# Probabilities of three attentions split in SBUF and turned by DMA, in pieces of 512 columns

## The chip, the cores and the metric

The kernel runs on one core of a Trainium2 chip. The metric is the device time of one execution in microseconds (us), from launch to the end. Engines named below: PE (TensorE, matrix products), DVE (VectorE), ACT (ScalarE), POOL (GpSimd) and SP, which here only issues DMAs. Each engine works through its own list of instructions in order, and semaphores tie the lists together.

## The reference

Two transformer layers over 1024 tokens of width 1024, all in float32. Layer 1 has two attentions, layer 2 has two more (one of them with three branches):

```python
# layer 1: y = rms_norm(x) @ w_in, split into the parts
oa = dsa_attention(...)          # A: every query keeps its 256 best keys by an index score
ob = swa_sink_attention(...)     # B: window of 128 keys, with a sink
x1 = x + concat([oa * silu(za), ob * silu(zb)]) @ w_out
# layer 2
oc = nsa_attention(...)          # C: compressed keys + selected keys + window of 512, gated sum
q  = (rms_norm(cq, d_q_lat_norm) @ d_w_uq); kv = (rms_norm(ckv, d_kv_lat_norm) @ d_w_ukv)
od = mla_attention(...)          # D: causal, 8 heads, q and kv from low-rank latents
out = x1 + concat([oc * silu(zc), od * silu(zd)]) @ w_out
# every attention:  p = exp(s - max);  o = (p / sum p) @ v,  8 heads in 2 groups of 4
```

## The kernel before, in words

Tokens are cut into 8 tiles of 128. Float32 precision on PE is kept by splitting an operand into a high and a low part and multiplying in passes: the projections take three matmuls per 128 rows (lines 498 to 500), the product of probabilities and values takes three matmuls with float16 parts (lines 690 to 692).

The generator `attn_gen` (lines 596 to 713) runs one job per query tile, group of four heads and branch. For each head it computes the scores into the PSUM tile `psS` (line 644), lets DVE add the mask, negate, store them to the SBUF tile `pt` and keep the row's extreme in `nm` (line 647), and lets ACT take the exponential with the sum (line 652). Then the probabilities, with queries on the partitions, have to be turned so that keys lie on the partitions. They are turned in groups of up to four 128x128 blocks (`tstage`): PE transposes each block into `psT` (line 672), and the group is split into float16 `ph` and `pl`, scaled by 4096, in one of two ways: "p", ACT copies PSUM to `ph` (line 676) and DVE subtracts for `pl` (line 677); or "q", ACT copies PSUM to the float32 tile `sg` (line 681) and POOL makes `ph` and `pl` (lines 682, 683). `WAYS` (line 72) gives the cycle of ways by attention and head group: entries 0 and 1 are B, 2 and 3 A, 4 and 5 C, 6 and 7 D. A head has one or two such groups (a head of 5 to 8 tiles has two; where there are fewer tiles, two or four heads share them). In all there are 390 groups: 30 in B, 86 in A, 188 in C, 86 in D. `cstage` (lines 685 to 697) then multiplies by the values. `tq` and `cq` hold back the turning and the product by one head or two, so that PE has other work in between.

Work of another kind is mixed in by `Lanes.run`: for each estimated nanosecond of attention ("main") it emits `ratio` ns of "fill", the projections of `fill_gen`, whose order in layer 2 is `FOO` (line 54) and whose rate in C is `CR` (line 44); D has a fill of its own (`d_fill`: queries, keys, values, the output product). During B the search for the 256 best keys of A runs beside it (`topk`, sixteen steps for the high half of the scores and sixteen for the low half, four ACT counts and two DVE counts each, line 851). A scheduler then puts the instructions in a final order on each engine, by its own estimate of when each can start; that order is fixed in the program. All DMAs of the kernel are issued by SP, in one list.

By time, in the profiled execution: until 160 us norm, first projections and index scores; 160 to 450 B, with the search; 450 to 620 A; 620 to 800 the first layer's output product and the first projections of layer 2; 800 to 1225 C with the other projections; 1225 to 1400 D, mostly its larger tiles; 1400 to 1543 the rest of D with the output product.

Of the kernel before, what the change touches and what calls it, by code (L numbers as in the profile page):

```python
# [10 lines left out]
F32 = mybir.dt.float32  # L11
# [11 lines left out]
P = 128  # L23
# [15 lines left out]
PSCALE = 4096.0  # L39
SLOT = 2048  # L40
# [3 lines left out]
CR = 0.75  # L44
DR = 0.8
WB = 2
XB = 2
# [6 lines left out]
FOO = 'ks kc kw qc0 zc0 zc1 cq qc1 zd0 zd1 ck'  # L54
# [13 lines left out]
PHB = 4  # L68
PTB = 3
CSB = 1  # L70
SG = 2
WAYS = ('q', 'q', 'ppq', 'pq', 'ppq', 'pq', 'ppq', 'p')
# [90 lines left out]
def trunk(ctx: ExitStack, tc: tile.TileContext, A, out):  # L163
# [377 lines left out]
    def v_scale(m, res):  # L541
# [17 lines left out]
        V.tensor_scalar(e[:, 0:1], e[:, 0:1], 2.0 ** -15 / PSCALE, None, op0=OP.mult)  # L559
# [36 lines left out]
    def attn_gen(jobs):  # L596
# [9 lines left out]
        for jb in jobs:  # L606
# [22 lines left out]
            for h0 in range(0, 4, per):  # L629
# [31 lines left out]
                if cmp_:  # L661
                    todo = [(2 * a, 0, a * P) for a in range(2)]
                for c in range(0, len(todo), 4):
# [3 lines left out]
                    def tstage(jb=jb, grp=grp, pt=pt, lastg=lastg, vh=vh, vl=vl, nk=nk, get_po=get_po, fin=fin, cmp_=cmp_,  # L667
                               fb=fbox if h0 + per == 4 else None):
# [4 lines left out]
                        ph = wk.tile([P, 4, P], F16, name="ph", bufs=PHB)  # L673
                        pl = wk.tile([P, 4, P], F16, name="pl", bufs=PHB)
                        if next(jb["way"]) == "p":
                            S.activation(ph[:, :n], pT[:, :n], AF.Copy, scale=PSCALE)  # L676
                            V.scalar_tensor_tensor(pl[:, :n], pT[:, :n], PSCALE, ph[:, :n], op0=OP.mult,  # L677
                                                   op1=OP.subtract)
                        else:
                            sg = wk.tile([P, 4, P], F32, name="sg", bufs=SG)  # L680
                            S.activation(sg[:, :n], pT[:, :n], AF.Copy, scale=PSCALE)  # L681
                            G.tensor_scalar(ph[:, :n], sg[:, :n], 1.0, 1.0, op0=OP.mult, op1=OP.mult)  # L682
# [1129 lines left out]
```

## Time and profile before

| | us |
|---|---|
| median of three timed runs (1543.71 to 1545.96) | 1545.52 |
| the profiled execution, device time | 1544.83 |
| its span, first to last instruction | 1542.8 |

| engine | busy, us | share of the span |
|---|---|---|
| PE | 1364.3 | 88% |
| DVE | 1110.0 | 72% |
| ACT | 919.6 | 60% |
| POOL | 874.4 | 57% |

The mean granted clock of TensorE was 0.946. A share over the whole span mixes stretches with different limits; so the stretches named above are read one by one.

### The profile page before, as it was taken

Reading aid. Unit: us, or ns where it says so; the run is one execution under the profiler, and the core shown is the slowest. Engines: PE = TensorE matmul, PEld = TensorE weight load, DVE = VectorE, ACT = ScalarE, POOL = GpSimd, SP = SyncE. Lnnn points to the kernel's source line nnn. Section 1 sums busy time; section 2 is a strip of 40 time slices with the busy share of each in tenths; the row PEclk is TensorE's granted clock in tenths of the full one; section 3 lists DMA queues with packets and bytes.
Section 4 is the critical chain, followed back from the end, with each engine's and each line's share of the span. In section 5 each row is a group of like instructions: output and inputs, shape, how many; then the busy total and the mean of one; then the engine's idle time right before and its main releaser. Section 6 shows DMA issues by size and latency. Waiting matters only on the chain.

```text
span 1542.8 us, 34986 instructions
## 1 busy us (share of the span) xinstructions
PE 1364.3 (88%) x12588; PEld 1261.3 (82%) x12588; DVE 1110.0 (72%) x3365; ACT 919.6 (60%) x2517; POOL 874.4 (57%) x1194
## 2 busy tenths in 40 slices
PE   5998899796418989999999999999998768789999
PEld 5988899696417778999999998899987557678887
DVE  5387775876797866248248668976689989987763
ACT  5355688898617856145424667857666676754531
POOL 6899654999748476225256443565456565652240
PEclk9999999898659999999999999999999879989999
DMA  6311223111002244132301210012001120111232
GB/s 201 93 31 34 67 70 87 30 36 61 7 28 73 68 107 128 44 132 63 91 21 53 59 47 8 16 52 60 29 12 41 57 68 13 32 52 63 93 114 75
DMA packets 88429, 93.18 MB, mean 60 GB/s; under 512 B 20928, under 2 KB 73152, under 8 KB 88256
## 3 DMA queue, kind: packets, MB, share of 16 engines
q1 hardware_dynamic: 88256, 90.95, 19.7%
q8 instruction: 99, 1.62, 0.4%
q14 instruction: 74, 0.61, 0.1%
HBM read 67.85 MB, written 23.07 MB: 59 GB/s over the span
## 4 chain that ended last, share of the span: by engine, by line
PE 53%; DVE 24%; ACT 8%; DMA 5%; issue 5%; POOL 4%; SPq 1%; POOLq 0%; DVEq 0%; ACTq 0%
PE pp L498 8%; PE pp L500 8%; PE pp L499 8%; PE psS L644 8%; PE psT L672 6%; ACT junka L851 4%; DVE pt L647 4%; PE pp L1697 2%; PE pp L1695 2%; PE pp L1696 2%; PE po L692 2%; PE po L690 2%; DVE pl L677 2%; PE po L691 2%; DMA wraw<-in_ab_w_in 1%
## 5 line engine op out<-in xcount | busy, mean ns | idle before, releaser
L498 PE MATMUL pp<-whi,Rh 128*128 128x256 f32 (+4 forms) x1648 | 483.4, 294 | 17.3 <-ACT sq L432 7.9
L499 PE MATMUL pp<-wlo,Rh 128*128 128x256 f32 (+4 forms) x1648 | 475.7, 289 | 1.7 <-POOL wlo L455 1.7
L500 PE MATMUL pp<-whi,Rl 128*128 128x256 f32 (+4 forms) x1648 | 476.4, 289 | 0.0
L652 ACT ACTIVATE pt<-pt,nm 128x256 f32<-128x256 f32 (+8 forms) x384 | 246.8, 644 | 169.2 <-DVE nm L647 165.0
L498 PEld LDWEIGHTS pp<-whi,Rh 128*128 128x128 f32 x1648 | 317.1, 193 | 23.7 <-ACT sq L432 9.5
L499 PEld LDWEIGHTS pp<-wlo,Rh 128*128 128x128 f32 x1648 | 316.8, 192 | 3.5 <-POOL wlo L455 2.3
L500 PEld LDWEIGHTS pp<-whi,Rl 128*128 128x128 f32 x1648 | 316.3, 192 | 1.2
L455 POOL TENSOR_TENSOR wlo<-wraw,whi 128x256 fp32r<-128x256 f32 (+4 forms) x208 | 164.6, 799 | 138.2 <-ACT whi L454 131.3
L672 PE MATMUL psT<-identf,pt 128*128 128x128 f32 x1256 | 215.2, 284 | 11.8 <-DVE pl L677 6.9
L682 POOL TENSOR_SCALAR ph<-sg 128x512 f16<-128x512 f32 (+3 forms) x157 | 88.1, 562 | 152.2 <-ACT sg L681 124.7
L683 POOL TENSOR_TENSOR pl<-sg,ph 128x512 f16<-128x512 f32 (+3 forms) x157 | 163.8, 1044 | 9.0
L672 PEld LDWEIGHTS psT<-identf,pt 128*128 128x128 f32 x1256 | 148.3, 144 | 24.0 <-DVE pl L677 8.8
L454 ACT ACTIVATE whi<-wraw 128x256 fp32r<-128x256 f32 (+4 forms) x208 | 83.8, 416 | 122.3 <-DMA wraw<-in_ab_w_in 38.0
L677 DVE SCALAR_TENSOR_TENSOR pl<-psT,ph 128x512 f16<-128x512 f32 (+3 forms) x233 | 128.0, 558 | 22.0 <-ACT ph L676 21.1
L676 ACT ACTIVATE ph<-psT 128x512 f16<-128x512 f32 (+3 forms) x233 | 111.5, 492 | 50.5 <-PE psT L672 44.2
L690 PEld LDWEIGHTS <-ph 128*128 128x128 f16 x1256 | 116.2, 99 | 22.3 <-issue 8.0
L692 PEld LDWEIGHTS <-pl 128*128 128x128 f16 x1256 | 114.0, 99 | 22.9 <-DVE pl L677 8.5
L647 DVE CUSTOM_DVE_ANT_0 pt<-psS,mk 128x512 f32<-128x512 f32 (+4 forms) x208 | 107.2, 520 | 27.4 <-PE psS L644 24.9
L691 PEld LDWEIGHTS <-ph 128*128 128x128 f16 x1256 | 116.4, 99 | 11.9 <-issue 10.6
L681 ACT ACTIVATE sg<-psT 128x512 f32<-128x512 f32 (+3 forms) x157 | 83.7, 535 | 43.1 <-PE psT L672 37.8
L644 PE MATMUL psS<-ka,qs 128*128 128x512 f32 (+4 forms) x192 | 57.4, 400 | 51.3 <-DVE nm L647 51.1
L644 PEld LDWEIGHTS psS<-ka,qs 128*128 128x128 f32 x192 | 32.9, 211 | 56.1 <-DVE nm L647 55.0
(311 smaller groups left out, 3588.3 us busy)
## 6 DMA issues: line engine op xcount, KB each, us to landing
wraw<-in_cd_w_in SPq DMA_DIRECT2D x72, 128.0 KB, 2.1
wraw<-in_ab_w_in SPq DMA_DIRECT2D x56, 128.0 KB, 2.1
xs<-in_x SPq DMA_DIRECT2D x8, 512.0 KB, 6.1
od<-mx SPq DMA_DIRECT2D x32, 128.0 KB, 1.8
wraw<-in_ab_w_out SPq DMA_DIRECT2D x32, 128.0 KB, 2.2
x<-in_x SPq DMA_DIRECT2D x8, 512.0 KB, 5.5
mo<-od SPq DMA_DIRECT2D x16, 256.0 KB, 2.7
nz<-zdr SPq DMA_DIRECT2D x16, 256.0 KB, 2.8
```

The source lines that it names most:

```text
L455: G.tensor_tensor(lo[:, :o], raw[:, :o], hi[:, :o].bitcast(F32), OP.subtract)
L498: T.matmul(ps, xh, hi[:, :n], start=q == 0 and k == 0, stop=False)
L499: T.matmul(ps, xh, lo[:, :n], start=False, stop=False)
L500: T.matmul(ps, xl, hi[:, :n], start=False, stop=q == 3 and k == 1)
L644: T.matmul(ps[:, at + a - c:at + b - c], lhs, rhs(a, b), start=n == 0, stop=n == len(pl_) - 1)
L647: V.tensor_tensor_reduce(pt[:, j * nk + c:j * nk + c + w], ps[:, at:at + w], mask(c, w), -1.0, first, op0=OP.add, op1=OP.min, accum_out=low)
L652: S.activation(pt[:, j * nk:(j + 1) * nk], pt[:, j * nk:(j + 1) * nk], AF.Exp, scale=-1.0, bias=nm[:, h:h + 1], accum_out=sm[:, h:h + 1])
L672: T.transpose(pT[:, a], pt[:, o:o + P], identf)
L677: V.scalar_tensor_tensor(pl[:, :n], pT[:, :n], PSCALE, ph[:, :n], op0=OP.mult, op1=OP.subtract)
L683: G.tensor_tensor(pl[:, :n], sg[:, :n], ph[:, :n], OP.subtract)
L690: T.matmul(dst, ph[:, a], vh(kt, h), start=kt == 0, stop=False)
L691: T.matmul(dst, ph[:, a], vl(kt, h), start=False, stop=False)
```

## The change

1. `WAYS` gets two new letters. In "d" and "g" the probabilities are split before they are turned: ACT copies up to 512 columns of `pt` to the first half of a float16 tile `hl`, DVE ("d") or POOL ("g") subtracts into its second half, and one DMA, issued by SP with `transpose=True`, turns all (up to eight) 128x128 blocks into `ht`. B takes "g" throughout, C alternates "d" and "g", D takes "dgg" in its first head group and "dg" in its second. A keeps "p" and "q" (now into `ht` too).
2. Buffers: four of `hl` (which `sg` shares) and four of `ht`, for two of `sg` and four each of `ph` and `pl`.
3. The scale 4096 is no longer applied when the group is split. Instead its logarithm is added to `nm` by one small ACT instruction before the exponentials of up to four heads; the sum carries the factor too, so it cancels in the division, and the factor goes from `v_scale`.
4. The estimated cost of turning is 1 ns in the new ways (110 ns a block in the old). `CR` goes from 0.75 to 1.2. `FOO` puts zd0 before qc1 and cq after it.
5. Memory is made: the two latent gains are no longer a row of 384 but three columns; they are multiplied into the small weights by ACT (`small_w`, six instructions) and not into the latents; `xr` shares buffers with `wraw2`.

The core of the diff:

```diff
-CR = 0.75
+CR = 1.2
-FOO = 'ks kc kw qc0 zc0 zc1 cq qc1 zd0 zd1 ck'
+FOO = 'ks kc kw qc0 zc0 zc1 zd0 qc1 cq zd1 ck'
-WAYS = ('q', 'q', 'ppq', 'pq', 'ppq', 'pq', 'ppq', 'p')
+WAYS = ('g', 'g', 'ppq', 'pq', 'dg', 'dg', 'dgg', 'dg')
...
+                S.activation(nm[:, h0:h0 + per], nm[:, h0:h0 + per], AF.Copy, bias=LNP)
                 for j, h in enumerate(hs):
                     S.activation(pt[:, j * nk:(j + 1) * nk], pt[:, j * nk:(j + 1) * nk], AF.Exp, scale=-1.0,
                                  bias=nm[:, h:h + 1], accum_out=sm[:, h:h + 1])
...
+                way, turned = [], []
+                for c in range(0, len(todo), 4):
+                    n = min(4, len(todo) - c)
+                    way.append(next(jb["way"]))
+                    ht = None
+                    if way[-1] in "dg":
+                        o, w = c * P, n * P
+                        hl = wk.tile([P, 1024], F16, name="hl", bufs=HLB)[:, :2 * w]
+                        S.activation(hl[:, :w], pt[:, o:o + w], AF.Copy)
+                        (V if way[-1] == "d" else G).tensor_tensor(hl[:, w:], pt[:, o:o + w], hl[:, :w], OP.subtract)
+                        ht = wk.tile([P, 8, P], F16, name="ht", bufs=HTB)
+                        nc.sync.dma_start(ht[:, :2 * n], hl.rearrange("p (k n) -> p k n", n=P), transpose=True)
+                    turned.append(ht)
...
-                        pT = tps()
-                        for a, (h, kt, o) in enumerate(grp):
-                            T.transpose(pT[:, a], pt[:, o:o + P], identf)
...
+                        if way in "pq":
+                            ht = wk.tile([P, 8, P], F16, name="ht", bufs=HTB)
+                            pT = tps()
+                            for a, (h, kt, o) in enumerate(grp):
+                                T.transpose(pT[:, a], pt[:, o:o + P], identf)
+                        ph, pl = ht[:, :n], ht[:, n:2 * n]
...
-                        return cstage, n * 110
+                        return cstage, n * 110 if way in "pq" else 1
...
+            S.activation(raw, raw, AF.Copy, scale=B["glat"][:, g + r:g + r + 1])
...
-            xr = D["pool"].tile([P, 512], F32, name="xr", bufs=XB)
+            xr = D["pool"].tile([P, 512], F32, name="xr", tag="wraw2", bufs=WB)
```

What this does to the lists of the engines, counted in their order: PE loses 968 of the 1256 transposes of line 672 (120 in B, 560 in C, 288 in D). SP's list grows from 546 to 850 DMAs, by 304 that turn: 196 of eight blocks, 16 of six, 44 of four and 48 of two. ACT gains 208 instructions on `nm` and six on the small weights. DVE's 233 splits become 131 "d" and 51 "p"; POOL's 157 pairs (lines 682, 683) become 173 single subtractions and 35 pairs.

PE, in the middle of C, before: scores of the window branch, then the four transposes of a group (`psT<-identf,pt`), then products with the values (`po`).

```order
L691 MATMUL po<-vls,ph 128x64
L644 MATMUL psS<-kw_10718,qs 128x320 x4
L672 MATMUL psT<-identf,pt 128x128 x4
L692 LDWEIGHTS pl
L692 MATMUL po<-vhs,pl 128x64
L690 LDWEIGHTS ph
L690 MATMUL po<-vhs,ph 128x64
```

The same part of C now:

```order
L707 MATMUL po<-vhw,ht 128x64
L645 MATMUL psS<-ks_9689,qs 128x512 x4
L705 LDWEIGHTS ht
L705 MATMUL po<-vhw,ht 128x64
L706 LDWEIGHTS ht
L706 MATMUL po<-vlw,ht 128x64
```

The transposes are gone from PE's list; what follows the scores now reads `ht`, which a DMA writes.

ACT, in C, before: exponentials (`pt,sm<-pt,nm`) beside copies out of `psT`.

```order
L652 ACTIVATE pt,sm<-pt,nm 128x640
L681 ACTIVATE sg<-psT 128x128
L652 ACTIVATE pt,sm<-pt,nm 128x64
L676 ACTIVATE ph<-psT 128x512
L676 ACTIVATE ph<-psT 128x128
```

ACT in C now, heads of 640 columns (`Rh<-wraw` splits a weight of the last product):

```order
L673 ACTIVATE hl<-pt 128x512
L673 ACTIVATE hl<-pt 128x128
L654 ACTIVATE pt,sm<-pt,nm 128x640
L1472 ACTIVATE Rh<-wraw_19056 128x512
L673 ACTIVATE hl<-pt 128x512
L652 ACTIVATE nm<-nm 128x1
L654 ACTIVATE pt,sm<-pt,nm 128x640
```

As many copies stand there as before, now from `pt`, and one `nm` instruction ahead of the exponential of each head.

SP, towards the end of C, before: weights of the last product and a store of C's result (`od_103<-cacc`).

```order
L1455 DMA wraw_19902<-in_cd_w_out 128x512
L1455 DMA wraw_19933<-in_cd_w_out 128x512
L1309 DMA od_103<-cacc 128x256
L1455 DMA wraw_19963<-in_cd_w_out 128x512
L1455 DMA wraw_19997<-in_cd_w_out 128x512
```

SP in that part of C now:

```order
L676 DMA_TRANSPOSE ht<-hl 128x8x128
L676 DMA_TRANSPOSE ht<-hl 128x2x128
L676 DMA_TRANSPOSE ht<-hl 128x4x128
L1471 DMA wraw_19123<-in_cd_w_out 128x512
L676 DMA_TRANSPOSE ht<-hl 128x8x128 x2
L1324 DMA od_103<-cacc 128x256
L676 DMA_TRANSPOSE ht<-hl 128x8x128 x2
L1471 DMA wraw_19153<-in_cd_w_out 128x512
```

The turning DMAs stand in one list with loads and stores, each behind whatever SP waits for next.

The fill of C moves as well. Cut C at every 32 of its 512 score matmuls on PE, into sixteen pieces: before, the last five hold 324 projection matmuls (95, 97, 0, 69, 63), now they hold 60 (18, 18, 0, 0, 24); the earlier eleven hold the others. At the end of the search, ACT's list before has the last four steps of the search with nothing else between their counts, now the last ten.

## Rows read from the trace of the kernel before

**Rows 1.** The page's parts 1, 2 and 4: busy time, 40 slices, chain.

```profile
PE 1364.3 (88%) x12588; PEld 1261.3 (82%) x12588; DVE 1110.0 (72%) x3365; ACT 919.6 (60%) x2517; POOL 874.4 (57%) x1194
...
PE   5998899796418989999999999999998768789999
DVE  5387775876797866248248668976689989987763
...
PE 53%; DVE 24%; ACT 8%; DMA 5%; issue 5%; POOL 4%; SPq 1%; POOLq 0%; DVEq 0%; ACTq 0%
```

**Rows 2.** Busy time of each engine by stretch (us, instruction counts in brackets).

```profile
core 0: us, PE busy (x) PEld busy (x) DVE busy (x) ACT busy (x) POOL busy (x), PEclk, DMA share, GB/s
160.00:450.00 290.00, 213.18 (x1875) 205.08 (x1873) 219.52 (x547) 216.03 (x592) 203.17 (x275) 0.87 0.16 46
450.00:620.00 170.00, 148.50 (x1662) 131.16 (x1663) 124.64 (x351) 111.38 (x267) 108.47 (x133) 0.93 0.31 92
800.00:1225.00 425.00, 409.37 (x4397) 384.99 (x4396) 338.34 (x1303) 276.88 (x841) 228.11 (x323) 0.99 0.14 40
1225.00:1400.00 175.00, 138.93 (x1216) 117.76 (x1215) 160.21 (x497) 113.93 (x290) 100.01 (x123) 0.87 0.13 41
1400.00:1543.00 143.00, 139.21 (x1028) 116.39 (x1026) 86.60 (x246) 55.07 (x138) 36.61 (x48) 1.00 0.28 90
```

**Rows 3.** Waits in 340:450, the search's end (us, times, longest).

```profile
DVE inc L866 <- ACT junka L851: 20.5, 13, 2.5
```

**Rows 4.** The same stretches, PE's transposes of line 672 alone.

```profile
160.00:450.00 290.00, 21.39 (x120) 14.03 (x120) 0.87 0.16 46
800.00:1225.00 425.00, 97.06 (x560) 65.36 (x560) 0.99 0.14 40
1225.00:1400.00 175.00, 29.52 (x183) 21.09 (x183) 0.87 0.13 41
1400.00:1543.00 143.00, 17.15 (x105) 12.29 (x105) 1.00 0.28 90
```

**Rows 5.** Stretch 640:680 (projections alone) and 960:1000 (no projections), all engines.

```profile
640.00:680.00 40.00, 40.00 (x340) 40.00 (x340) 8.84 (x25) 9.81 (x22) 12.19 (x16) 1.00 0.27 87
960.00:1000.00 40.00, 39.57 (x515) 35.17 (x515) 37.51 (x150) 36.55 (x108) 21.13 (x27) 1.00 0.03 9
```

**Rows 6.** Durations by line, ns min/median/max.

```profile
L723 ACT ACTIVATE es<-es x16: 189/196/253, 175.3 to 339.2; 128x4 f32<-128x4 f32 x16
L851 ACT ACTIVATE junka<-lo,cand x64: 709/878/1078, 303.4 to 415.8; 128x512 int8<-128x512 uint16 x16, 128x640 int8<-128x640 uint16 x16, 128x768 int8<-128x768 uint16 x16, 128x896 int8<-128x896 uint16 x16
L364 DVE TENSOR_TENSOR nz<-nz,rp_t x27: 680/691/1700, 70.6 to 1041.0; 128x512 f32<-128x512 f32 x27
L677 DVE SCALAR_TENSOR_TENSOR pl<-psT,ph x233: 260/678/693, 462.4 to 1517.0; 128x512 f16<-128x512 f32 x74, 128x128 f16<-128x128 f32 x19, 128x256 f16<-128x256 f32 x17, 128x384 f16<-128x384 f32 x7
L676 ACT ACTIVATE ph<-psT x233: 254/577/677, 461.1 to 1516.3; 128x512 f16<-128x512 f32 x74, 128x128 f16<-128x128 f32 x19, 128x256 f16<-128x256 f32 x17, 128x384 f16<-128x384 f32 x7
L683 POOL TENSOR_TENSOR pl<-sg,ph x157: 421/1163/1730, 179.5 to 1370.3; 128x512 f16<-128x512 f32 x121, 128x128 f16<-128x128 f32 x16, 128x256 f16<-128x256 f32 x16, 128x384 f16<-128x384 f32 x4
```

**Rows 7.** Stretch 800:1225, line 677 (DVE's split) alone.

```profile
800.00:1225.00 425.00, 58.11 (x110) 0.99 0.14 40
```

**Rows 8.** Stretch 960:1000, instructions that touch psS (scores).

```profile
960.00:1000.00 40.00, 17.56 (x67) 10.16 (x66) 17.02 (x35) 0.00 (x0) 1.00 0.03 9
```

**Rows 9.** Stretch 960:1000, line 672 (transposes) alone.

```profile
960.00:1000.00 40.00, 15.83 (x96) 10.90 (x96) 1.00 0.03 9
```

**Rows 10.** DMA: the queue's total, and issues with KB and us to landing.

```profile
q1 hardware_dynamic: 88256, 90.95, 19.7%
mo<-od SPq DMA_DIRECT2D x16, 256.0 KB, 2.7
g<-in_b_qk_norm SPq DMA_DIRECT2D x2, 32.0 KB, 3.6
```

**Rows 11.** Waits of the SP queue (us in total, times, longest).

```profile
SPq L1309 <- POOL cacc L1307: 147.7, 15, 22.6
```

More of the change, by code (lines that the diff above doesn't have):

```diff
@@ L39 @@
 PSCALE = 4096.0
+LNP = float(np.log(PSCALE))
+HLB = 4
+HTB = 4
 SLOT = 2048
@@ L665, in attn_gen, with tstage @@
                     lastg = h0 + per == 4 and c + 4 >= len(todo)
-                    def tstage(jb=jb, grp=grp, pt=pt, lastg=lastg, vh=vh, vl=vl, nk=nk, get_po=get_po, fin=fin, cmp_=cmp_,
-                               fb=fbox if h0 + per == 4 else None):
+                    def tstage(grp=grp, pt=pt, lastg=lastg, vh=vh, vl=vl, nk=nk, get_po=get_po, fin=fin, cmp_=cmp_,
+                               fb=fbox if h0 + per == 4 else None, way=way[c // 4], ht=turned[c // 4]):
                         n = len(grp)
-                        pT = tps()
-                        for a, (h, kt, o) in enumerate(grp):
-                            T.transpose(pT[:, a], pt[:, o:o + P], identf)
[L673 to L682, printed above, removed]
-                            G.tensor_tensor(pl[:, :n], sg[:, :n], ph[:, :n], OP.subtract)
@@ new lines, in tstage @@
+                        if way in "pq":
[4 more added lines that the diff above has]
+                        ph, pl = ht[:, :n], ht[:, n:2 * n]
+                        if way == "p":
+                            S.activation(ph, pT[:, :n], AF.Copy)
+                            V.tensor_tensor(pl, pT[:, :n], ph, OP.subtract)
+                        elif way == "q":
+                            sg = wk.tile([P, 4, P], F32, name="sg", tag="hl", bufs=HLB)
+                            S.activation(sg[:, :n], pT[:, :n], AF.Copy)
+                            G.tensor_scalar(ph, sg[:, :n], 1.0, 1.0, op0=OP.mult, op1=OP.mult)
+                            G.tensor_tensor(pl, sg[:, :n], ph, OP.subtract)
@@ L1342, in lat_pre, with lat_chain @@
         D["kx"] = ks_[:, 1024:2048].rearrange("p (a b n) -> p a b n", a=2, b=2)
-        B["glat"] = cc.tile([P, 384], F32, name="glat")
-        nc.sync.dma_start(B["glat"][:, 0:256], row(A["d_q_lat_norm"][0], 0, 256))
-        nc.sync.dma_start(B["glat"][:, 256:384], row(A["d_kv_lat_norm"][0], 0, 128))
+        B["glat"] = cc.tile([P, 3], F32, name="glat")
+        nc.sync.dma_start(B["glat"][:, 0:2], A["d_q_lat_norm"][0].rearrange("(k p) -> p k", p=P))
+        nc.sync.dma_start(B["glat"][:, 2:3], A["d_kv_lat_norm"][0].rearrange("(k p) -> p k", p=P))
         G.tensor_scalar(B["glat"], B["glat"], RG, 1.0, op0=OP.mult, op1=OP.mult)
-    def lat_chain(z, ss, n, g, dst):
+    def lat_chain(z, ss, n, dst):
         yield
@@ L1362, in lat_chain, with lat_start @@
         L.give("psT")
-    def lat_start(ps, n, g, dst):
+    def lat_start(ps, n, dst):
         L.take("nz", NZ)
@@ L1459, in wout_gen, with small_w @@
                     yield
-    def small_w(ap, rows, n, tag):
+    def small_w(ap, rows, n, tag, g):
         hi = D["pool"].tile([P, rows, n], F32R, name="wh" + tag)
@@ L1557, in next_query @@
         if (i, g) == (0, 0):
-            D["wuq", 1] = small_w(wq[:, 384:768], 2, 384, "q")
+            D["wuq", 1] = small_w(wq[:, 384:768], 2, 384, "q", 0)
     def d_prologue():
@@ L1747, in trunk @@
             L.tick()
-    D["wkv", 1] = small_w(wkv[:, 512:1024], 1, 512, "kv")
+    D["wkv", 1] = small_w(wkv[:, 512:1024], 1, 512, "kv", 2)
     FD = d_fill()
```

19 lines of the change are left out of this document (8 added, 11 removed).

## The prediction, made before the changed kernel ran

> **What bounds the kernel now.** I read the page first. PE is busy 88% of the span, and the chain of waits runs through PE for 53% and DVE for 24% [rows 1]. The slices show that this isn't one regime: in the last third PE's digits fall to 6 and 7 where DVE's rise to 9. So I went to the busy times by stretch [rows 2]. From 800 to 1225 us (C) PE is busy 409 of 425 us and DVE 338: PE bounds it. From 1225 to 1400 (first part of D) DVE is busy 160 of 175 and PE 139: DVE bounds it, and the granted clock falls to 0.87. From 1400 on PE is busy 139 of 143. From 160 to 450 (B and the search) nobody is busy over 76%: the search is a chain, DVE waiting for ACT's counts [rows 3]. Then I took the same stretches for line 672 alone [rows 4]: the transposes that leave PE take 21 us in B, 97 in C, 30 and 17 in D. Last I compared a stretch of projections alone with one of C without projections [rows 5]. The first is PE alone (340 matmuls in 40 us, 0.118 us each). In the second PE is full (39.6 of 40), but DVE (37.5) and ACT (36.6) are close behind it. That decides what C can win.
>
> **The change part by part.** The profiled execution took 1544.8 us (span 1542.8, 2.0 around it), 0.7 below the median; the terms are added to 1544.8.
>
> *B, 160 to 450.* 21 us of PE go, from a stretch that PE doesn't bound; the split moves from two POOL instructions to one, and ACT keeps one copy per group. ACT gains 16 of the `nm` instructions at 0.196 us (the nearest row, ACT on 128x4 [rows 6]): 3 us. ACT's list now ends the search with ten steps alone, four before; a step needs the same ACT work there as beside B, so what is added at the end leaves the part before it. I take **+3 us**. At worst that part gets no shorter: a step is four counts of 0.88 us [rows 6] and a wait of 20.5 / 13 = 1.6 [rows 3], 5.1 us, so six more make +31; at best −10, half of PE's 21.
>
> *A, 450 to 620.* The turning stays. 44 `nm` instructions stand between DVE's extreme and the exponential, 44 x 0.196 = 9 us. ACT is busy 111 of 170 there [rows 2], so part of it falls into waiting anyway: I take **+4 us** (0 to 9).
>
> *C, 800 to 1225.* PE's 409 us become 312. DVE has 94 splits where it had 110; the new one reads two SBUF operands instead of PSUM, for which the nearest row is line 364, 691 ns at 512 columns against 678 now [rows 6], so the price stays, and 16 x 0.53 (the mean in C is 58.1 us / 110 [rows 7]) leave: 338 becomes 329. ACT gains 104 x 0.196 = 20: 277 becomes 297. So C can't go below DVE's 329 / 0.963 (PE's density there now) = 342, a gain of 83. It will not reach that, because the fill has moved. In C without projections 40 us hold 67 score matmuls [rows 8], so a sixteenth of C (32) takes 19.1 us. Of PE's 39.6 us there 15.8 are transposes [rows 9]; 23.7 remain, 11.3 per sixteenth. The last five sixteenths hold 60 projections now: PE 5 x 11.3 + 60 x 0.118 = 64 us in all. They don't get shorter, since DVE needs 17.9 us of each 19.1 and ACT 17.5 + 6.5 x 0.196 = 18.7. Here the four `hl` buffers come in too: one is held from ACT's copy through the subtraction until the DMA has landed, 0.58 + 0.69 to 1.16 us [rows 6] + landing. The trace has no turning DMA; the nearest landings are 2.7 us (256 KB, the size of a full piece) and 3.6 us for rows of 256 bytes [rows 10], which is the length of a row of a 128-column block in float16. With 3.6 and two pieces per head, four buffers give a head each (3.6 + 1.5) / 2 = 2.55 us against 19.1 / 8 = 2.38 now, so 20.4 per sixteenth: 102 us. The first eleven hold the rest of PE's work, 312 − 64 = 248 us; at density 0.963 that is 258. Together 360: **−65 us**. From it I take back **15 us** for what a longer chain costs where nothing stands ahead: the first groups of B, C and D and the last of D (landing 3.6 us each, in place of four transposes), and SP's list, where a turning DMA stands behind a store whose producer is late (now up to 22.6 us in line 1309 [rows 11], harmless as long as nobody waits behind it).
>
> *D, 1225 to 1543.* Its DVE splits fall from 72 to 36, 19 us at the same 0.53; half lies in the part that DVE bounds: **−10 us**. In the last part PE is the bound and loses 17 us [rows 4], while DVE has 56 us to spare: **−15 us**, leaving two for the drain. ACT gains 44 x 0.196 = 9 us against 61 us of slack or more in either part. Both ends: 0 if the output product waits for the last heads anyway, −37 if all counts.
>
> *The rest.* The gain columns cost six ACT instructions (some 4 us) and make DVE's 16 latent multiplications shorter; the weights are loaded while PE is busy with C, so they are hidden, and at worst cost 4 us. The removed scale changes no instruction's length.
>
> Sum: +3 + 4 − 65 + 15 − 10 − 15 = −68, and 1544.8 − 68 = **1477 us**. The spread of the terms without a change of regime is 1455 to 1510.
>
> DMA is what I can't see. The pieces carry 968 blocks x 2 x 32 KB = 63.4 MB. The queue now moves 90.95 MB in 19.7% of 1542.8 us [rows 10], 0.299 MB per us. By bytes the turning costs 212 us, 123 of it in C beside the 60 us (0.14 of 425) that are there now: 183 of 360, hidden. The other end is in the second rival.
>
> Rows of the profile have no transposing DMA at all. The Trainium skill speaks both ways: "Advanced Engine Details and Errata", section X-Bar Transpose (TRN2), puts them at the speed of ordinary DMAs; "VectorE: DVE Perf Modes", section The three transpose paths, gives 1309 ns for one 128x128 block by DMA against 390 ns on TensorE, and its rules say to use TensorE where PSUM will do as a target. The trace has PE's block at 0.17 us (97 us / 560). If blocks went one by one at the page's price, C's 1120 would need an estimated 1466 us; if the 1309 ns are mostly the fixed part of a DMA, as 2.7 us for a whole 256 KB here suggest, the page is no objection; by its first reading the second rival is right, and worse than I price it.
>
> **The rivals.**
> *The full gain.* The scheduler's order in C hides the landings, the five late sixteenths run at DVE's pace, and C takes 342 us; D gives 27: 1544.8 + 7 − 83 − 27 = 1442. For it: DVE reached 37.5 of 40 us in C. Against it: ACT would have to be as dense. Chance 0.13 (1430 to 1455).
> *Turning is slower than PE's work: slower than before.* The DMA engines pay by row of 256 bytes, not by byte. Now a packet takes 0.197 x 1542.8 x 16 / 88256 = 0.055 us [rows 10]. The pieces have 968 x 2 x 128 = 247,808 such rows; at the same price 852 us, 493 of them in C. With the 60 us of loads C takes 553 in place of 425: 1544.8 + 128 = 1673, with nothing gained in D (253 + 63 of 318 us). It decides from (360 − 60) / 123 = 2.4 times the price by bytes, and makes the kernel slower from (425 − 60) / 123 = 3.0 times. For it: 32 KB in rows of 256 bytes land after 3.6 us, 256 KB in long rows after 2.7. Against: those rows cross from HBM, and 16 engines had 86% idle time in C. Chance 0.22, spread from 1550 to 1680.
> *Little gain.* PE's time comes back as waits for buffers: with landing 6.3 us, four `hl` buffers pass 188 pieces at (6.3 + 1.5) / 4 = 1.95 us each, 367 us for C if evenly spread, but the dense heads (two pieces each) then take 3.9 us, not 2.38: 40 heads in the late part lose 61 us. C gives −65 + 61, D −25: 1544.8 + 7 − 29 = 1523, up to no change. Chance 0.18 (1510 to 1548).
>
> **How the numbers follow.** Forecast 0.47 (1455 to 1510, about 1477), full gain 0.13, little gain 0.18, slower 0.22. Runs of this kernel tell a difference of 0.2%, 3 us, from none. Faster: 0.47 + 0.13 + 0.14 of the third; same: 0.03 of the third; slower: 0.22 and 0.01 of the third. The range leaves out half of the full gain (below 1440) and somewhat over half of the slower case (above 1580).
>
> **What would show it.** Right: C about 360 us long, PE near 312 us in it and still the fullest in its first two thirds, DVE and ACT over 17 of each 19 us at its end, landing of `ht` 3 to 4 us, DMA share in C below 0.6; D's second part some 15 us shorter. Wrong by the second rival: landing over 8 us, PE's products (line 705) waiting for DMA for tens of us, DMA share near 1 or pieces issued one after the other's end. Wrong by the third: ACT's copies (line 673) waiting for `ht` DMAs. The search's end later than 450 us by more than 10 would show that I priced its ten lone steps too low.

## The result, and the profile after

The changed kernel takes 1583.0 us (median of 4 runs, 1578.6 to 1586.6) against 1545.7 for the kernel before: ratio 1.0248, 95% interval 1.0230 to 1.0266. It is 37 us slower where 68 us less were forecast. The two profiled executions (1586.6 and 1544.8 us) are 42 us apart, and most of it arises in two places: the search ends at 427.6 us instead of 416.8 (start of ACT's last count); C, from its first score to its last product, takes 441 us instead of 401. From there to the end it takes 308 instead of 317, which gives 9 back. A takes 2 us less than before.

The page's parts 1 to 3 after the change (the last line: a DMA queue's packets, MB and share of 16 engines' span):

```profile
PE 1316.5 (83%) x11620; PEld 1193.0 (75%) x11620; DVE 1117.4 (71%) x3314; ACT 959.1 (61%) x2731; POOL 864.7 (55%) x1123
...
PE   5998999975028999999999988989867667778998
...
DVE  5387765886697866167356557986997689987772
...
PEclk8999999988559999999999999989967668869999
...
q1 hardware_dynamic: 345920, 154.23, 43.0%
```

PE has lost 968 instructions but only 48 us of busy time [rows 1]. From 1149 us on (slice 30 of 40) PE's digits fall to 6 and 7, in C and not only in D, and the granted clock falls with them, to 0.6 to 0.8 (a value between 0.5 and 1 is a mean over its two levels, 1.2 and 2.4 GHz). Before, after the search, only three slices from 1196 us on were below 0.9:

```profile
PEclk9999999898659999999999999999999879989999
```

Busy times by stretch, columns as in [rows 2], each stretch shifted to the same work:

```profile
160.00:460.00 300.00, 199.64 (x1759) 191.57 (x1757) 219.09 (x547) 220.54 (x608) 183.56 (x246) 0.85 0.32 71
460.00:630.00 170.00, 149.91 (x1657) 130.11 (x1658) 123.47 (x352) 118.80 (x311) 107.78 (x132) 0.92 0.30 90
811.00:1276.00 465.00, 397.85 (x3859) 356.46 (x3858) 359.24 (x1328) 303.57 (x967) 218.13 (x267) 0.89 0.60 116
1276.00:1420.00 144.00, 100.27 (x803) 82.89 (x801) 130.60 (x394) 97.59 (x272) 91.75 (x107) 0.76 0.52 109
1420.00:1585.00 165.00, 152.90 (x1130) 126.02 (x1129) 104.76 (x273) 72.10 (x184) 64.83 (x78) 0.98 0.59 139
```

In C PE is idle for 67 of 465 us (16 of 425 before [rows 2]). I expected 312 us of PE work there; 398 are shown. No engine has taken PE's place as the bound: DVE is at 77%, ACT at 65%. What PE waits for, in the same stretch (us, times, longest; a weight load, PEld, and its matmul can wait for the same thing, so the lines overlap):

```profile
PEld psS L645 <- DVE nm L648: 41.1, 53, 3.6
PEld L705 <- DMA ht<-hl: 39.6, 50, 2.5
...
PE psS L645 <- DVE nm L648: 28.9, 36, 3.5
ACT hl L673 <- DMA ht<-hl: 27.1, 30, 2.2
PE po L705 <- DMA ht<-hl: 26.9, 36, 2.1
```

The turning DMA itself (ns min/median/max of SP's time for one issue; then us to landing):

```profile
L676 SPq DMA_TRANSPOSE ht<-hl x304: 1167/1232/2353, 181.7 to 1566.2; - x152
...
DMA to landing us min/median/max: 2.3/3.2/5.2
```

It lands after 3.2 us, close to the 3.6 assumed. But SP spends 1.23 us on every issue, where an ordinary one takes about 0.33 (16 weight loads of line 1455 before: 0.327 to 0.333). SP's list in the late part of C, where heads follow each other without fill (start, us, count):

```profile
1205.47 22.55 SPq L676 DMA_TRANSPOSE ht<-hl  x16
1228.07 0.57 SPq L1324 DMA_DIRECT2D od<-cacc  x1
1228.74 16.63 SPq L676 DMA_TRANSPOSE ht<-hl  x12
```

Here SP does nothing but issue, 1.4 us apart; over the whole of C it issues for 0.67 of the time. A head with two pieces costs SP 2.8 us; before, a head took 2.38. And the same scores are slower on PE. In this stretch, 1195 to 1245, those of 320 columns take 445 ns in the mean, where C before had 345 (now, then before):

```profile
L645 PE MATMUL psS<-kw,qs 128*128 128x320 f32 x32 | 10.9, 445 | 3.0 <-DVE nm L648 2.8
...
L644 PE MATMUL psS<-kw,qs 128*128 128x320 f32 x128 | 32.5, 345 | 1.5 <-DVE nm L647 1.4
```

### The profile page after: what moved, and what is told of

It reads as the page before. It is cut to its first block, busy times and chain, and to the rows that moved or that the text cites. A ratio compares the mean times of both kernels' runs of the same rounds, so it can differ in the third digit from the quotient of the medians.

```text
span 1584.8 us, 33892 instructions
## 1 busy us (share of the span) xinstructions
PE 1316.5 (83%) x11620; PEld 1193.0 (75%) x11620; DVE 1117.4 (71%) x3314; ACT 959.1 (61%) x2731; POOL 864.7 (55%) x1123
## 5 line engine op out<-in xcount | busy, mean ns | idle before, releaser
L674 POOL TENSOR_TENSOR hl<-pt,hl 128x512 f16<-128x512 f32 (+3 forms) x173 | 179.8, 1043 | 170.2 <-ACT hl L673 145.1
L705 PEld LDWEIGHTS <-ht 128*128 128x128 f16 x1256 | 121.0, 104 | 87.1 <-DMA ht<-hl 62.7
L673 ACT ACTIVATE hl<-pt 128x512 f16<-128x512 f32 (+3 forms) x304 | 155.6, 539 | 35.3 <-DMA ht<-hl 32.1
L652 ACT ACTIVATE nm<-nm 128x1 f32<-128x1 f32 (+2 forms) x208 | 41.6, 201 | 156.1 <-DVE nm L648 155.3
L707 PEld LDWEIGHTS <-ht 128*128 128x128 f16 x1256 | 122.2, 104 | 9.4 <-POOL ht L698 5.3
L706 PEld LDWEIGHTS <-ht 128*128 128x128 f16 x1256 | 123.3, 105 | 5.8 <-issue 5.3
L674 DVE TENSOR_TENSOR hl<-pt,hl 128x512 f16<-128x512 f32 (+3 forms) x131 | 94.8, 724 | 26.8 <-ACT hl L673 26.3
L645 PE MATMUL psS<-kd,qhl 128*128 128x512 f32 (+4 forms) x192 | 59.7, 394 | 19.3 <-DVE nm L648 17.6
L654 ACT ACTIVATION_READ_ACCUMULATOR pt<-pt,nm 128x1 f32 x384 | 73.1, 190 | 0.0
L645 PE MATMUL psS<-ks,qs 128*128 128x512 f32 (+4 forms) x192 | 64.2, 432 | 6.2 <-DVE nm L648 5.9
```

Of the source, the lines that this page charges most:

```text
L645: T.matmul(ps[:, at + a - c:at + b - c], lhs, rhs(a, b), start=n == 0, stop=n == len(pl_) - 1)
L673: S.activation(hl[:, :w], pt[:, o:o + w], AF.Copy)
L674: (V if way[-1] == "d" else G).tensor_tensor(hl[:, w:], pt[:, o:o + w], hl[:, :w], OP.subtract)
L705: T.matmul(dst, ph[:, a], vh(kt, h), start=kt == 0, stop=False)
L706: T.matmul(dst, ph[:, a], vl(kt, h), start=False, stop=False)
L707: T.matmul(dst, pl[:, a], vh(kt, h), start=False, stop=kt == nt - 1)
```

## The experiments

All times are medians; each ratio is to the kernel before, with its interval. "C" is from its first score to its last product, "clock" the mean granted clock of TensorE in the profiled execution. The theories were numbered as they came up: 1, SP's time for each issue; 2, the fill's move; 3, 4 and 5, PE's density and clock, the lead of a turned piece, the clock with SP relieved. The plain copies (e20, e21, e23, e24) leave the turning out: the products then read the probabilities as they lie.

| run | us | ratio, 95% interval | C, us | clock |
|---|---|---|---|---|
| changed kernel | 1583.0 | 1.0248 (1.0230 to 1.0266) | 441 | 0.899 |
| e1_c_on_pe | 1568.3 | 1.0151 (1.0122 to 1.0180) | 444 | 0.934 |
| e2_all_on_pe | 1566.4 | 1.0136 (1.0121 to 1.0151) | 444 | 0.941 |
| e5_two_issues | 1839.4 | 1.1900 (1.1878 to 1.1922) | 618 | 0.832 |
| e8_one_per_head | 1597.4 | 1.0344 (1.0317 to 1.0370) | 449 | 0.898 |
| e3_old_fill | 1602.0 | 1.0362 (1.0329 to 1.0395) | 448 | 0.899 |
| e12_pe_old_fill | 1558.0 | 1.0083 (1.0053 to 1.0114) | 411 | 0.946 |
| e4_no_nm | 1578.8 | 1.0215 (1.0185 to 1.0245) | 439 | 0.903 |
| e13_pe_no_nm | 1552.5 | 1.0044 (1.0026 to 1.0062) | 439 | 0.944 |
| e14_pe_turns_too | 1611.5 | 1.0442 (1.0414 to 1.0470) | 453 | 0.935 |
| e15_longer_lead | 1620.0 | 1.0498 (1.0462 to 1.0534) | 473 | 0.888 |
| e17_five_buffers | 1613.8 | 1.0448 (1.0411 to 1.0484) | 470 | 0.892 |
| e18_c_half | 1576.6 | 1.0211 (1.0177 to 1.0245) | 446 | 0.917 |
| e20_plain_copy | 1554.7 | 1.0061 (1.0038 to 1.0084) | 428 | 0.906 |
| e21_plain_in_four | 1830.4 | 1.1846 (1.1829 to 1.1864) | 610 | 0.830 |
| e11_act_issues | 1887.5 | 1.2222 (1.2202 to 1.2242) | 671 | 0.825 |
| e23_plain_and_pe | 1585.2 | 1.0283 (1.0264 to 1.0303) | 444 | 0.935 |
| e24_plain_old_no_nm | 1544.3 | 1.0011 (0.9994 to 1.0029) | 411 | 0.911 |
| e6_small_on_pe | 1580.2 | 1.0252 (1.0233 to 1.0272) | 450 | 0.914 |

**Turning back on PE: all of it, and C alone.**

```diff
-WAYS = ('g', 'g', 'ppq', 'pq', 'dg', 'dg', 'dgg', 'dg')
+WAYS = ('q', 'q', 'ppq', 'pq', 'ppq', 'pq', 'ppq', 'p')   # e2
+WAYS = ('g', 'g', 'ppq', 'pq', 'ppq', 'pq', 'dgg', 'dg')  # e1
```

> All four attentions turn on PE with the ways of before; only the nm instructions, the split buffers, the gain columns, the fill's order and rate are as changed. Theory 1 (turning by DMA costs the time): 1546 to 1556, that is before plus what 208 nm instructions of 0.2 us put on the path (0 to 10 us). Rival (fill and nm): above 1570. The search's end comes back from 427.6 to about 417 us in either, as B's turning leaves SP and ACT's list.

> C's probabilities go back to PE's transposes and the split after them (ways ppq and pq); B, D, the order and rate of the fill, the nm instructions and the buffers stay as changed. C took 401 us before and 441 after, by the first score and the last product of C in the two traces. Theory 1 (C is held up by the turning itself: SP's list, which spends about 1.23 us on each turning DMA, and the longer way to PE): C comes back to 401 to 410 us and the whole to 1540 to 1553, with PE's products no longer waiting for DMA in C. Rival (the fill that was moved ahead is to blame: the last five sixteenths of C have nothing to cover their waits): C stays above 425 and the whole above 1567. Rival (the nm instruction in the chain from DVE's extreme to the exponential): C stays near 420 to 430.

e2 lies between the two sides, e1 came out as the fill's rival said. The rest of the change costs 21 us by itself (e2); turning by DMA adds 17, 15 of them by C's ways. C's length says little here: it is 444 with the transposes and 441 without, with as many projections in it (1394 matmuls), but in e1 and e2 the first 18 and 19 of D's scores already stand in it. The search's end in e2 is 421.8, not the 417 expected in either case.

**Fill and nm, on PE and by DMA.**

```diff
-CR = 1.2                                              # e3; e12, with e2's ways
+CR = 0.75
-FOO = 'ks kc kw qc0 zc0 zc1 zd0 qc1 cq zd1 ck'
+FOO = 'ks kc kw qc0 zc0 zc1 cq qc1 zd0 zd1 ck'
-S.activation(nm[:, h0:h0 + per], nm[:, h0:h0 + per], AF.Copy, bias=LNP)   # e4; e13, with e2's ways
```

> The changed kernel with the fill's rate and order of before (CR 0.75, cq ahead of zd0). With all turning back on PE the new rest still cost 21 us (1566 against 1545), and turning by DMA adds 17 to it. Theory 2 (those 21 us are the fill's move, and the two add up): 1558 to 1567. Rival (turning by DMA is a gain that the moved fill hides, because the waits of the late heads of C have nothing beside them): 1500 to 1540. Rival (the nm instructions cost the 21 us): stays at 1578 to 1586.

> All turning on PE and the fill's rate and order of before: what is left of the change is the nm instructions, the buffers, the gain columns. Theory 2 (the fill's move costs the 21 us): 1545 to 1551, C back from 444 to about 401 us. Rival (nm): 1560 to 1567 and C stays above 420.

> The changed kernel without the 208 nm instructions, so without the factor 4096 in the probabilities. I priced them at +4 us in A and at nothing in C. Theory 2: 3 to 8 us less, 1575 to 1581. Rival (the instruction lengthens the chain from DVE's extreme to the exponential at every head, and the wait that shows at it, 67 us in C, is its doing): 1555 to 1566.

> All turning on PE, the fill as changed, without the nm instructions and the factor 4096. Theory 2 (the fill's move costs the 21 us): 1556 to 1563, C still above 430 us. Rival (nm): 1543 to 1550, C near 405.

Only e4 came out as theory 2 said; e12 and e13 lie between the sides, each with a part of the 21 us. With turning on PE the nm instructions cost 14 us (e2 to e13) and the moved fill 8 (e2 to e12): I had priced nm at 4 and the fill as a loss only for the DMA's version. With turning by DMA it is the other way round: nm costs 4, hardly more than the spread of the changed kernel's runs, and the old fill would cost 19 more. So the moved fill, which e1 seemed to blame, costs some 8 us, and only with turning on PE. Theory 2 thus fell in the form that the parts add up: e3 went to 1602 where 1558 to 1567 was expected. In e3 the scores of C without fill come in one block earlier (945 to 1025 us), and there SP issues 43 turning DMAs in 65 us without a pause worth naming.

**SP's time per issue.**

```diff
-nc.sync.dma_start(ht[:, :2 * n], hl.rearrange("p (k n) -> p k n", n=P), transpose=True)
+for u in range(2):                                     # e5: two issues, half the blocks each
+    nc.sync.dma_start(ht[:, u * n:(u + 1) * n],
+                      hl[:, u * w:(u + 1) * w].rearrange("p (k n) -> p k n", n=P), transpose=True)
...
+nc.sync.dma_start(ht[:, :2 * n], hl.rearrange("p (k n) -> p k n", n=P))      # e20: a plain copy
...
+for u in range(0, P, 32):                              # e21: a plain copy in four
+    nc.sync.dma_start(ht[u:u + 32, :2 * n], hl[u:u + 32].rearrange("p (k n) -> p k n", n=P))
...
+(nc.sync if way[-1] == "d" else nc.scalar).dma_start(..., transpose=True)    # e11
```

> Each turning DMA is issued as two of half its blocks: 608 issues, the same blocks and bytes, the same buffers. Theory 1 (SP's time per issue, 1.23 us whatever the size, sets C's pace): two more issues per head of two pieces add about 2.5 us to each of the 40 late heads of C and 1.2 us to many others, so C gets 60 to 150 us longer and the whole 1640 to 1780. Rival (bytes, landing or four buffers set the pace): the bytes are the same and a half lands no later than the whole, so the time stays within 10 us of 1583. If SP's time on an issue goes with its size, the same.

> Every turning DMA becomes a plain one of the same bytes from hl to ht (nothing is turned, so the products use the probabilities as they lie). Everything else of the change stays: split, buffers, nm, fill; only the scheduler's order differs a little, since it prices the two DMAs differently. Theory 1 (SP's 1.23 us for each turning DMA holds up the heads that have no fill beside them): a plain issue takes 0.33 to 0.43 us, SP is no longer full, the 64 scores of C from 256 to 320 take under 36 us (48 with turning DMAs, 27 on PE with the same fill), PE's waits at line 705 fall from 108 to under 50 us, and the whole takes 1505 to 1550. Rival (the longer chain through split, DMA and four buffers): 1570 to 1590.

> As the plain copy, but each in four DMAs of 32 partitions: the same bytes, four plain issues of 0.33 to 0.43 us, 1.3 to 1.7 us of SP per piece, as a turning DMA takes. Theory 1 (SP's time per piece): the time comes back to 1565 to 1610, and C's dense heads to 2.8 us each. Rival (the turning itself, its 256-byte packets and their landing): within 12 us of the plain copy.

> The changed kernel; the pieces that POOL splits (173 of 304) are issued from ACT's list, the others from SP's. SP's list gets half as long in C. Theory 1 (SP's list is the bound where heads follow each other without fill): if an issue costs ACT little, 1540 to 1565. If an issue takes 1.2 us of ACT as it does of SP, ACT gets some 115 us more in C beside its 292, and waits in order for POOL: 1590 to 1650. Either way the waits at line 705 for pieces from SP fall. Rival (landing, not SP): 1575 to 1590 with the same landing of 3.2 us.

SP's issues of e5, e20 and e21 in this order, ns min/median/max:

```profile
L677 SPq DMA_TRANSPOSE ht<-hl x608: 1106/1207/2775, 180.0 to 1821.6; - x152
```

```profile
L676 SPq DMA_DIRECT2D ht<-hl x304: 464/471/1457, 182.6 to 1537.0; - x152
...
DMA to landing us min/median/max: 1.8/2.3/5.9
```

```profile
L677 SPq DMA_DIRECT2D ht<-hl x1216: 507/588/1951, 182.3 to 1807.4; - x174
```

All four moved the way theory 1 said, each by another amount: e5, e21 and e11 lost more than expected (a plain issue of a quarter takes 0.59 us, not 0.33 to 0.43), e20 gained less. An issue costs SP 1.2 us whatever the size of the piece: half the blocks, the same time. 608 x 1.21 = 735 us (e5) and 1216 x 0.59 = 715 us (e21) of SP's list cost the same total, 1839 and 1830, though e21 turns nothing and moves no 256-byte rows. In C SP issues for 0.84 (e5) and 0.81 (e21) of the time, 0.67 in the changed kernel. That shows SP's list as a bound where it is as long as in these two, whatever its DMAs do; for the changed kernel, where it is full in stretches only, they don't show it.

The plain copy (143 us of SP, not 375) takes 28 us off the changed kernel, with the fill where it stood: that is what turning costs against copying. How much of it is SP's list isn't told apart; a part can be the landing (2.3 for 3.2 us) or the DMA engines' own time (176 for 378 us). And where SP's list is fullest it gained no more than elsewhere: C from its 353rd score of 512 on takes 130 us in e20, 134 in the changed kernel. Of the 28 us 9 come from C before that, 11 from behind C and 4 from ahead of it. So with issues of 0.47 us in place of 1.23 that late part is hardly faster. This stretch of e20 (columns as in [rows 2]):

```profile
1129.80:1259.70 129.90, 96.12 (x895) 75.82 (x895) 108.42 (x376) 94.69 (x269) 71.36 (x75) 0.70 0.45 153
```

PE's waits at line 705, of weight loads and products together, fall from 108 to 52 us.

In e11 ACT takes as long for an issue as SP does (1.25 us, some 220 us of its list in all): PE's weight loads at line 705 wait 312 us for pieces, 63 in the changed kernel. 1887 is far more than the 1590 to 1650 expected: here ACT, which also computes, was no place for these issues.

**Fewer issues.**

```diff
+hl = wk.tile([P, 2048], F16, name="hl", bufs=2); hw = wk.tile([P, 16, P], F16, name="ht", bufs=2)  # e8, once per head
+nc.sync.dma_start(hw[:, :2 * nb], hl[:, :2 * nb * P].rearrange(...), transpose=True)  # after both subtractions
...
+if n == 1 and way[-1] in "dg":                         # e6
+    way[-1] = "p"
...
+WAYS = ('g', 'g', 'ppq', 'pq', 'dq', 'gp', 'dgg', 'dg')   # e18
```

> One turning DMA for all of a head's blocks (up to sixteen with the two halves) in place of two; two buffers of double size in place of four. About 195 issues in place of 304, the same blocks and bytes; a head's first product now waits for the subtraction of the whole head. Theory 1 (SP's time per issue): late heads of C spend 1.3 us of SP in place of 2.8, SP is no longer full, C falls from 441 to 400 to 420 and the whole to 1540 to 1565. Rival (landing, chain length and buffers): fewer buffers and a longer chain per head, so the time stays or grows, 1583 to 1640. If SP's time goes with the size, an issue takes about 2.5 us and the time does not fall.

> The changed kernel, but a piece of a single block goes PE's way: 48 turning DMAs of two blocks fewer, 256 in place of 304, 3% of the turned bytes. Theory 1 (SP's time per issue): 48 x 1.25 = 60 us less of SP, two thirds of it where C's heads follow each other without fill: 1563 to 1576. Rival (bytes, landing, chain): 1579 to 1586.

> In C every second group is turned by DMA and the others on PE (ways dq and gp), so 210 turning DMAs in place of 304, and PE keeps half of the transposes between the products. Theory 3 (density of PE): C's late part keeps a clock over 0.9, the time is below both kinds of C alone, 1545 to 1565 against 1583 and 1568. Rival (each turning DMA costs its share, some 0.08 us a piece of the 15 us between them): in the middle, 1570 to 1580.

e8 and e6 missed theory 1's numbers and e18 theory 3's; the rivals held. One DMA per head lowers SP's issues to 164 of 1.44 us, but a piece then lands after 4.0 us, has to wait for the whole head's split and finds two buffers only: 14 us slower than the changed kernel. 48 small issues fewer gain 3 us at most, inside the interval. Half of C on PE gains 6. So SP's list explains what happens when it is made longer (e5, e21) and may explain the 28 us of the plain copy, but shortening it a little doesn't give time in proportion.

**Density, lead and buffers.**

```diff
+else:                                                  # e14; e23, with the plain copy
+    pT = tps()
+    for a, (h, kt, o) in enumerate(grp):
+        T.transpose(pT[:, a], pt[:, o:o + P], identf)   # nobody reads pT
...
-HTB = 4; PTB = 3
+HTB = 6; PTB = 2   # e15, which also doubles tlag in C and D
+HLB = HTB = 5; PTB = 2   # e17
```

> The changed kernel, in which PE also transposes every group that the DMA turns, into psT, and nobody reads that. PE so does the work of before again (97 us in C, 21 in B, 47 in D) on top. Theory 3 (where C's heads are dense, PE waits a little at each product and score, the granted clock falls to 0.6 to 0.8 there, and the score matmuls get longer: the freed time goes into slower matmuls): PE stays dense, the clock in the late part of C stays at 0.95 or more, and the time falls or stays in spite of the added work, 1560 to 1583. Rival (the chain through SP and landing sets the pace whatever the clock): the added work comes on top of unchanged waits, 1595 to 1680.

> The plain copy (1555 us), in which PE also transposes every group of C, D and B into psT, and nobody reads that: SP is relieved and PE is kept as busy as before. In the plain copy PE is idle for a fifth of C's late part, and the granted clock there is 0.64 to 0.68, so a score matmul takes 0.44 to 0.54 us instead of 0.31 to 0.39. Theory 5 (what is left of the freed PE time is lost to this clock): PE stays at 0.95 or more, the added work fits into the idle time and the time is 1535 to 1560, although PE does 968 transposes more. Rival (the chain from score to exponential to split sets the pace whatever the clock): the added work lengthens it, 1565 to 1600.

> The changed kernel with the products of C and D held back by one head more (lag of the queue doubled), six buffers ht in place of four, two of pt in place of three. Theory 4 (PE's waits at line 705 for a turned piece, 108 us in the whole run, come from a lead of one head that is too short for split, issue and landing): these waits fall under 40 us, the clock in C rises and the time falls to 1535 to 1565. Rival (SP's issues and the chain of scores set the pace): the waits move to the scores and to ACT's copies, 1575 to 1600.

> The changed kernel with five buffers each of hl and ht in place of four, two of pt in place of three, lag as it was. My third rival (buffers): ACT's waits for ht DMAs (32 us) fall under 10 and the time falls by 8 to 25 us, to 1558 to 1575. Rival: the pieces wait for SP instead, 1578 to 1590; if two of pt are too few, more.

With PE's transposes back beside the DMA the mean granted clock returns from 0.899 to 0.935, but the time grows by 28 us (e14), and by 31 with the plain copy (e23). Both came out as the rivals said: theories 3 and 5 fell as they stood, though the clock in C's late part rose to 0.90 and 0.88 only, not to the 0.95 that they asked for. These two runs measure something else: 968 transposes put back on PE cost 28 to 31 us. But not the transposes alone, since the scheduler moved fill with them. Matmuls of projections from C's 353rd score of 512 to its last product, in the changed kernel and in e14 (stretch and its length, busy us, count; then clock, DMA share, GB/s):

```profile
1142.20:1276.50 134.30, 10.26 (x42) 0.67 0.70 134
...
1129.00:1283.50 154.50, 52.43 (x356) 0.90 0.62 115
```

e23 has some 360 there, the plain copy alone 42, and e3, which moves only the fill, cost 19. So how much of the 28 to 31 is the transposes' own stays open. The busy totals on the page of e14, and the group of the added transposes (count, busy us, mean ns, idle before):

```profile
PE 1380.6 (86%) x12588; PEld 1273.6 (79%) x12588; DVE 1122.4 (70%) x3314; ACT 960.1 (60%) x2731; POOL 869.7 (54%) x1123
```

```profile
L693 PE MATMUL psT<-identf,pt 128*128 128x128 f32 x968 | 168.6, 289 | 8.4 <-ACT pt L654 3.7 <-DVE kd L1523 2.9 <-DVE krs L1432 0.9
```

The added transposes show as 169 us of busy time, and PE's total grows by 64 (from 1316.5). e15 and e17 paid for their buffers with one of three `pt`, and both lost over 30 us (e15 more than either side expected), with ACT's waits for buffers down to 17 and 6 us. PE's waits at line 705 rose to 133 and 132 us, where theory 4 expected under 40. So here a `pt` buffer is worth more than one of `hl` or `ht`; a longer lead with three `pt` is not tried.

**Everything favourable at once.** The plain copy, the old fill, no nm instructions (edits as above): the best case of the change, which leaves out the turning and the factor 4096.

> The plain copy with the fill's rate and order of before and without the nm instructions (and so without the factor 4096): the split ahead of the turn with as little else as the kernel allows. Theory 1 plus the chain: with SP relieved, C's heads without fill still run at the lower clock, 1535 to 1555, no faster than before by more than 10. Rival (nm and the fill hid the gain that I forecast): 1480 to 1520.

1544.3 us, ratio 1.0011 (0.9994 to 1.0029): no change, as theory 1 with the chain said, with 968 transposes fewer on PE and an issue at 0.47 us. The stretch 945 to 995, C without fill, of this run (columns as in [rows 2]):

```profile
945.00:995.00 50.00, 39.54 (x424) 28.87 (x424) 43.22 (x141) 40.99 (x103) 23.62 (x24) 0.83 0.45 159
```

PE 79%, DVE 86%, ACT 82%, at a clock of 0.83. Before, such a stretch had 99, 94 and 91% at full clock [rows 5]. None of these engines is full. No run beat the kernel before.

## Why the prediction was wrong, point by point

**The step that failed is C's 360 us**: PE's work falls from 409 to 312, the last five sixteenths take 102 at the pace of the buffers, and the rest 258 "at density 0.963". The same work took 465. The stretch up to C's 353rd score of 512 and the last five sixteenths, now and (below) before, columns as in [rows 2]:

```profile
811.00:1142.20 331.20, 298.74 (x2972) 278.82 (x2970) 252.26 (x962) 211.36 (x706) 157.97 (x203) 0.97 0.56 109
1142.20:1276.50 134.30, 99.57 (x893) 77.93 (x893) 107.44 (x368) 92.69 (x262) 60.15 (x65) 0.67 0.70 134
...
800.00:1096.90 296.90, 294.31 (x3107) 280.39 (x3105) 226.00 (x824) 192.54 (x580) 154.06 (x208) 1.00 0.15 42
1096.90:1225.80 128.90, 115.86 (x1308) 105.16 (x1305) 113.14 (x482) 84.34 (x262) 74.85 (x116) 0.97 0.11 35
```

The first part took 331 us for 258: PE is busy for 299 where 248 were reckoned, and idle for 32 where 10 were. The last five sixteenths took 134 for 102: PE is busy for 100 instead of 64 and idle for 35. So 73 of the 105 us missed lie where the granted clock is 0.97; the slow clock, 0.67, belongs to the last five alone. Three errors stand in this step.

1. *The freed time was too large.* I took line 672's busy time by stretch, 97 us for 560 [rows 4]. But the records of matmuls overlap: the next starts before the last one ends. PE's timeline in the kernel before (start, us):

```profile
962.72 1.07 PE L672 MATMUL psT<-identf,pt 128*128 128x128 f32 x8
963.55 0.54 PE L644 MATMUL psS<-kw,qs 128*128 128x320 f32 x2
...
964.42 0.66 PE L672 MATMUL psT<-identf,pt 128*128 128x128 f32 x4
964.91 0.19 PE L692 MATMUL po<-vhs,pl 128*128 128x64 f16 x1
```

From start to start eight take 0.83 us and four 0.49: 0.10 to 0.12 each, not 0.17. That is some 62 us in C (560 x 0.11) and 106 in all where I reckoned 165. In the first part, with 360 of the 560, it is some 23 of the 51 us by which PE's work was reckoned too small; where the other 28 come from isn't traced.

2. *An engine's free time is not time.* I let PE keep its density with its transposes gone. With the cheap issue of e20 C takes 428, and in e24 411, while PE, DVE and ACT all have time to spare. That the loop over engines (score, mask and extreme, exponential, split, DMA, product; each engine's list in fixed order, three `pt`) sets the pace, with PE's transposes standing between its links before, is my reading of this; no run shows it by itself. Going on from e2 (1566) the three measured steps are: transposes kept on PE, but the products fed through split and plain copy, +19 (e23); transposes off PE, −31 (e20); turning instead of copying, +28 (the changed kernel). Before e2 come 14 for nm and 7 for fill and the rest, together 21. That it adds up to the 37 proves nothing, since each step starts where the one before ends. The steps are differences of medians with intervals of some 4 us each, they depend on order, as nm's 14 against 4 shows, and in the +19 and the −31 the fill in C moves too.

3. *SP's issue had no price.* I took a DMA's cost from its landing and its bytes, and from SP's list only that a turning DMA may stand behind a store. 304 x 1.23 = 375 us of a list that has to be in order was visible nowhere in the trace before, but the price of an ordinary issue was. What turning costs against copying, the issue and all else, is the 28 us of e20, of which 4 lie in C's last five sixteenths, where SP's list is fullest.

**The terms.** B, +3: the search's end moved by 10.8, inside my −10 to +31. My sign measured it from 450 us, the end of the stretch; the search itself ended at 416.8 before. The sign blamed the ten lone steps. But without nm and with plain copies (e24) the search ends at 418.9, and with turning on PE nm alone moves it from 416.6 to 421.8 (e13, e2), so they are not alone in it. A, +4: from the search's end to A's last product 198 us, 200 before; nothing. D, −25: from C's last product to the end −9; in e24 −11. With the old fill it takes 322 us both with turning by DMA (e3) and on PE (e12): there D gained nothing. The last 165 us have PE busy for 153, less dense than before [rows 2], and in the 144 us ahead of them the granted clock is 0.76, 0.87 before. The fill: I charged its move as a loss for the DMA's version, and e3 shows a gain of 19. `nm`: 203 ns by median as priced; but the sum had 7 us of it, in B and A, and with turning on PE it was worth 14. DVE's split: pieces of 512 columns take 797 ns in the mean and up to 1754, where I kept the old price, and the old split took 685 and never passed 693 [rows 6]; why isn't tested.

**The second rival** said slower, 1550 to 1680, and one of its signs is there: PE's products waiting for DMA for tens of us. The others are not: the landing is 3.2 us, not over 8, the DMA share isn't near 1, and pieces are issued 1.4 us apart, before the one ahead has landed. So it has the time by luck: its mechanism isn't the one. The turning packets took (0.430 x 1584.8 − 0.197 x 1542.8) x 16 / 257,664 = 0.023 us each, not 0.055, in all 378 us: 1.8 times the price by bytes, below the 2.4 from which it would decide. The queue that the trace shows is in SP's list, not in the DMA engines, whose share in C is 0.60.

**The third rival**'s sign is there too (ACT waiting for `ht` DMAs, 27 us in C), but more buffers at the cost of a `pt` made it worse; with `pt` untouched it stays open.

The prediction weighed two pages. The Trainium skill, "VectorE: DVE Perf Modes", section Rules for kernel authors, names TensorE for a transpose of 128x128 where PSUM will do. That pointed the right way here. The Trainium skill, "VectorE: DVE Perf Modes", section The three transpose paths, gives 1309 ns for one bf16 block by DMA. That is no price for each block here: pieces of two to eight float16 blocks land after 3.2 us by median. The Trainium skill, "Advanced Engine Details and Errata", section X-Bar Transpose (TRN2), puts turning DMAs at the speed of ordinary ones. That is not borne out: 1.23 us per issue for 0.47, 3.2 us to land for 2.3, and 378 us of the DMA engines for 176, with the same bytes. The Trainium skill, "Perfetto Trace Analysis", section What "DMA-bound" means, lists the issuing engine's sequencer, its track solid with DMA slices, as a bound apart from the DMA engines. SP's rows from 1205 to 1245 show such a track, and e5 and e21 what it costs; but the plain copy, with issues of 0.47 us, made C's last five sixteenths, where these rows lie, only 4 us shorter.

**What stays open.** How the clock and the chain share the loss in C's late part. The slower matmuls are shown (445 for 345 ns), and that raising the clock with idle work gains nothing; but that work takes PE's time too and moved the fill, so the runs don't tell the two apart. And in the earlier part, at nearly full clock, the 32 us that PE waits and the 28 us of longer work are shown, but no run takes them away one by one.

## What to carry to other kernels

Value freed work by what the loop can use, not by an engine's busy share. Put the work back unread and look at the time, and look too at what else moved: here 968 matmuls of 0.11 us, with the fill that moved beside them, cost some 30 us. Read the price of matmuls that overlap from start to start. Where a change adds DMAs, count the issues on the list that issues them, with the time per issue of that kind of DMA, before counting bytes. That a list looks full doesn't yet say what shortening it gives: here issues of 0.47 us for 1.23 gave 4 of 134 us where the list was fullest.

## What the runs showed of the hardware

- A turning DMA of two to eight blocks takes SP 1.2 us to issue (least 1167 ns, median 1232; 1207 with half pieces), a plain one of the same tiles 0.47 us.
- ACT's list pays the same: 1.25 us for each.
- Turning 63.3 MB, in 247,808 packets of 256 bytes, took 378 us of all 16 DMA engines, copying them plainly 176 us (0.308 x 1556.7 − 0.197 x 1542.8).
